# Sums of squares in one tile: DVE adds in place of products with the ones, in eight norm boundaries of a two-block transformer kernel

## Chip, cores and metric

The kernel runs on one core of one Trainium2 chip. The metric is the device time of one execution in microseconds. The kernel before has a median of 3141.66 us over three runs (3138.09 to 3142.01).

PE is the matrix engine (TensorE), DVE the vector engine, ACT the scalar engine, POOL is GpSimd; SP issues the DMAs. Each engine carries out its own instructions in the order in which the program put them, and waits where one of them needs something that another engine has not finished.

## What is computed

Two blocks of two layers each work on 512 tokens of width 1024. Each layer is a mixer and then an FFN, with a norm ahead of each and a norm behind it. The mixers (attention over chosen keys beside a chunked mLSTM in block 1; compressed, selected and windowed attention beside stick-breaking attention in block 2) play no part in the change. What matters is the frame around them:

```python
def rms_norm(x, w):
    y = x * lax.rsqrt(jnp.mean(x * x, axis=-1, keepdims=True) + EPS)
    return y * w

for l in range(DEPTH):
    h = rms_norm(x, mix_norm_pre[l]) * (1.0 + sc_m) + sh_m
    y = hybrid_mixer(h, ...)
    x = x + g_m * rms_norm(y, mix_norm_post[l])
    h = rms_norm(x, ffn_norm_pre[l]) * (1.0 + sc_f) + sh_f
    y = swiglu(h, w_gate_up[l], w_down[l])
    x = x + g_f * rms_norm(y, ffn_norm_post[l])
```

Block 2 has the same frame without scale, shift and gate (`sc`, `sh`, `g`). So between two stages there stands a boundary: the norm of y (the stage's result), the addition to x, and the norm of x for the next stage. There are eight boundaries: four after mixers and four after FFNs. The last one has no norm of x, since nothing follows it.

## The kernel before

Activations are kept with the features on the partitions: x is eight tiles of 128 features by 512 tokens in 32-bit floats, and so is y. Each weight product is done as three: the weights and the activations are split into a high part and a low part, and high by high, low by high and high by low are summed (`mm3`, which calls `self.matmul`, L303). In the views, `whi` and `wlo` are the parts of a weight: `load` fetches it by a DMA on SP, ACT copies it to `whi` (L263) and DVE subtracts to make `wlo` (L265), 128x1024 or less at a time. `hh` and `hl` are the parts of the normed x.

A mean over the features is a sum over the partitions and over eight tiles. The sum over the partitions is a product with a 128x128 tile of ones, `nrm<-...,ones` in the views, which leaves the sum on all 128 partitions. Each such product is recorded as two passes.

At a boundary the tokens are worked in two halves of 256 (`HALVES`), so that the first half can be normed while PE works on the second half of the stage's last products:

- `out_proj` (after a mixer) and `down2` (after an FFN) make y tile by tile. For each tile the square is taken on ACT (`sqy`) and added by DVE into a running tile `ssy`, except for the last of the eight tiles, whose square stays in its own tile `sql`. After a mixer ACT copies y and squares it straight from PSUM (L514, L516); after an FFN DVE first adds y to an earlier part (L1098) and ACT squares the sum (L1100).
- `post_norm` (L485) takes one half. One product with the ones over `ssy` and one over `sql` give the sum of squares of y; ACT turns it into `rstd` by Ln and Exp (L273); DVE then makes eight `yn` (L498) and adds them to x (L499).
- `squares` (L443) follows for the same half: ACT squares the eight tiles of x (L448), DVE adds them in pairs (L450), which leaves four tiles.
- `pre_norm` (L455) takes the four tiles by four products with the ones, makes `rstd` on ACT, and then `xn` on DVE (L468), `hh` on ACT (L470 or L472) and `hl` on DVE (L478 or L483).
- `norms` sets where these steps stand among the products of the stage: the first half's norm of y at the start of the second half's products, the first half's norm of x `LA` = 4 (mixer) or `LB` = 3 (FFN) weight tiles later, the second half's norm of y behind the last of them. The second half's norm of x is put off into the next stage (`self.pending`, run in `fm_split`), behind the first of its weight tiles.

The framework's scheduler gives the final order on each engine from priorities. `load` raises the priority of its DMA, its copy and its subtraction (`high_priority`), so that weights' copies come to stand between the steps of a norm. Tile names carry a number in the orders below.

Of the kernel before, what the change touches and what calls it, by code (L numbers as in the profile page):

```python
# [14 lines left out]
ALU = mybir.AluOpType  # L15
# [26 lines left out]
PH1 = 0  # L42
PH2 = 0
PXM = 0
SA = 0
LA = 4
LAG = 3
LOA = 40
# [136 lines left out]
class Net:  # L185
# [256 lines left out]

    def squares(self, hs):  # L443

        nc, x, res = self.nc, self.x, []
        for k in range(KT):
            s2 = self.half("sq")
            nc.scalar.activation(s2, x[k][:, hs], AF.Square)  # L448
            if k % 2:
                nc.vector.tensor_tensor(s2, res[-1], s2, ALU.add)  # L450
                res.pop()
            res.append(s2)
        return res

    def pre_norm(self, hs, sqs, gs, sh, hh, hl):  # L455

# [28 lines left out]
    def post_norm(self, hs, y, sqs, g, end=False):  # L485

        nc = self.nc
        ps = self.ps("nrm")
        if SA:
            nc.vector.tensor_tensor(sqs[0][:, hs], sqs[0][:, hs], sqs[1][:, hs], ALU.add)  # L490
# [1260 lines left out]
```

## Time and profile before

| | |
|---|---|
| median of 3 runs | 3141.66 us (3138.09 to 3142.01) |
| profiled execution | 3140.83 us |
| its span on the core | 3139.1 us |
| PE busy | 97%, 16196 instructions |
| DVE busy | 64%, 3692 instructions |
| ACT busy | 49%, 2758 instructions |
| mean granted clock of PE | 0.984 |

The span is what the profiler saw between the first and the last instruction. Busy time of one engine overlaps with that of the others. A timeline row gives the start in us from the span's start, the time that the instruction took (or a run of equal ones, with their count after the x), the engine, line and operation, what is written from what, and in brackets how long the engine had been idle before it and which instruction ended that. The granted clock is told as a part of full speed: 1.00 is 2.4 GHz, 0.50 is 1.2 GHz.

### The profile page before, as it was taken

How to read it: one execution, taken by the hardware profiler on the slowest of the kernel's cores; microseconds unless marked ns; L12 is line 12 of the kernel's file. 1: busy time of each engine (PE TensorE's matmuls, PEld its weight loads, DVE VectorE, ACT ScalarE, POOL GpSimd, SP SyncE). 2: the span in 40 equal slices, each digit the busy share in tenths (PEclk: the TensorE clock that was granted, in tenths of full speed). 3: DMA queues.
4: the chain of work that ended last, by engine and by line, in shares of the span. 5: the costliest groups of instructions: out<-in, count | busy, mean ns of one | idle time of the engine just before them, and what ended most of it. 6: DMA issues, size and time to landing. Idle time of an engine off the chain costs nothing.

```text
span 3139.1 us, 42582 instructions
## 1 busy us (share of the span) xinstructions
PE 3033.7 (97%) x16196; PEld 2533.5 (81%) x16196; DVE 2012.8 (64%) x3692; ACT 1545.5 (49%) x2758; POOL 66.7 (2%) x179
## 2 busy tenths in 40 slices
PE   7998999999999999999999999999999999999998
PEld 6774788889875798888988779888898877898887
DVE  6888575547787572336677677735576766775465
ACT  4445642235445652324477655534455866554343
POOL 0000000000000000000000100000000001000000
PEclk8997999999998999999999999999999999999999
DMA  7344366645322232324411124333343112342323
GB/s 236 96 137 167 101 222 196 208 141 163 112 93 69 87 125 85 110 84 158 127 61 41 61 69 151 109 97 101 97 163 107 35 48 74 114 135 83 113 82 110
DMA packets 118925, 358.40 MB, mean 114 GB/s; under 512 B 15408, under 2 KB 28464, under 8 KB 118720
## 3 DMA queue, kind: packets, MB, share of 16 engines
q1 hardware_dynamic: 118720, 355.68, 34.8%
q8 instruction: 127, 2.08, 0.3%
q14 instruction: 78, 0.64, 0.1%
HBM read 336.19 MB, written 8.42 MB: 110 GB/s over the span
## 4 chain that ended last, share of the span: by engine, by line
PE 68%; issue 17%; DVE 10%; ACT 3%; DMA 1%; POOL 1%; SPq 0%; POOLq 0%; DVEq 0%; ACTq 0%
PE ps L303 29%; PE op L303 12%; PE pj L303 9%; PE dn L303 8%; PE po L303 3%; PE tk L303 2%; DVE wlo L265 2%; PE nrm L303 1%; PE pt L306 1%; DVE yn L498 1%; DVE ss L1495 1%; DVE x L499 1%; DVE ia L846 1%; ACT whi L263 1%; DVE m L845 1%
## 5 line engine op out<-in xcount | busy, mean ns | idle before, releaser
L265 DVE TENSOR_TENSOR wlo<-raw,whi 128x1024 fp32r<-128x1024 f32 (+1 forms) x562 | 628.6, 1123 | 556.4 <-ACT whi L263 553.4
L263 ACT ACTIVATE whi<-raw 128x1024 fp32r<-128x1024 f32 (+1 forms) x562 | 549.4, 980 | 779.9 <-PE ps L303 210.7
L303 PE MATMUL ps<-hh,wlo 128*128 128x512 f32 (+1 forms) x1560 | 570.6, 366 | 0.2 <-DVE wlo L265 0.2
L303 PE MATMUL ps<-hl,whi 128*128 128x512 f32 (+1 forms) x1560 | 570.8, 367 | 0.1
L303 PE MATMUL ps<-hh,whi 128*128 128x512 f32 (+1 forms) x1560 | 570.3, 367 | 0.0
L303 PE MATMUL pj<-hh,whi 128*128 128x512 f32 (+1 forms) x944 | 352.9, 375 | 15.9 <-ACT hh L670 8.4
L303 PE MATMUL pj<-hl,whi 128*128 128x512 f32 (+1 forms) x944 | 351.4, 373 | 6.5 <-DVE hl L478 3.4
L303 PE MATMUL pj<-hh,wlo 128*128 128x512 f32 (+1 forms) x944 | 350.7, 372 | 0.0
L303 PEld LDWEIGHTS ps<-hh,wlo 128*128 128x128 f32 x1560 | 294.1, 189 | 48.7 <-DVE wlo L265 1.0
L303 PEld LDWEIGHTS ps<-hl,whi 128*128 128x128 f32 x1560 | 294.2, 189 | 48.5 <-DVE hl L478 0.4
L303 PEld LDWEIGHTS ps<-hh,whi 128*128 128x128 f32 x1560 | 293.2, 189 | 48.7 <-ACT whi L263 0.4
L303 PEld LDWEIGHTS pj<-hh,whi 128*128 128x128 f32 x944 | 179.4, 191 | 55.3 <-ACT hh L670 10.4
L303 PEld LDWEIGHTS pj<-hl,whi 128*128 128x128 f32 x944 | 180.2, 191 | 36.7 <-DVE hl L478 4.4
L303 PEld LDWEIGHTS pj<-hh,wlo 128*128 128x128 f32 x944 | 180.2, 191 | 30.1 <-issue 1.2
L649 DVE CUSTOM_DVE_ANT_0 wm<-wm,cact 128x1024 f32<-128x1024 f32 x96 | 117.0, 1222 | 107.2 <-DMA wm<-in_w_mod_dram 106.7
L303 PE MATMUL op<-hidh,wlo 128*128 128x256 f32 (+1 forms) x572 | 176.8, 309 | 1.4 <-DVE wlo L265 1.4
L303 PE MATMUL op<-hidh,whi 128*128 128x256 f32 (+1 forms) x572 | 177.1, 310 | 0.0
L303 PE MATMUL op<-hidl,whi 128*128 128x256 f32 (+1 forms) x572 | 175.8, 307 | 0.0
L303 PE MATMUL dn<-hidh,whi 128*128 128x512 f32 x352 | 136.9, 389 | 0.0
L303 PE MATMUL dn<-hidl,whi 128*128 128x512 f32 x352 | 136.9, 389 | 0.0
L303 PE MATMUL dn<-hidh,wlo 128*128 128x512 f32 x352 | 136.9, 389 | 0.0
L273 ACT ACTIVATE p<-p,st 128x128 f32<-128x128 f32 (+3 forms) x192 | 106.2, 556 | 56.0 <-DVE st L888 36.8
(350 smaller groups left out, 5782.8 us busy)
## 6 DMA issues: line engine op xcount, KB each, us to landing
raw<-in_w_in_dram SPq DMA_DIRECT2D x134, 512.0 KB, 3.4
raw<-in_w_up_dram SPq DMA_DIRECT2D x100, 512.0 KB, 3.5
wm<-in_w_mod_dram SPq DMA_DIRECT2D x96, 512.0 KB, 4.5
raw<-in_w_gu_dram SPq DMA_DIRECT2D x94, 512.0 KB, 3.5
raw<-in_w_dn_dram SPq DMA_DIRECT2D x80, 512.0 KB, 3.6
raw<-in_w_out_dram SPq DMA_DIRECT2D x52, 512.0 KB, 3.6
raw<-in_w_dn_dram SPq DMA_DIRECT2D x80, 192.0 KB, 3.2
hp<-rp SPq DMA_DIRECT2D x96, 64.0 KB, 2.0
```

What stands on the lines that cost most here:

```text
L263: nc_.scalar.activation(hi[:, :n], raw[:, :n], AF.Copy)
L265: (self.lo_eng or nc_.vector).tensor_tensor(lo[:, :n], raw[:, :n], hi[:, :n].bitcast(F32), ALU.subtract)
L273: j = self.nc.scalar.activation(out, in_, func, **kw).ins
L303: return self.paced(self.nc.tensor.matmul(*args, **kw))
L306: return self.paced(self.nc.tensor.transpose(*args))
L498: nc.vector.scalar_tensor_tensor(t, y(k, hs), g[:, k:k + 1], r, ALU.mult, ALU.mult)
L499: (nc.gpsimd if PXM >> k & 1 else nc.vector).tensor_tensor(self.x[k][:, hs], self.x[k][:, hs], t, ALU.add)
L649: self.nc.vector.tensor_tensor_reduce(raw, raw, self.cact, 1.0, 0.0, ALU.mult, ALU.add, self.mod[l][:, c:c + 1])
L845: nc.vector.max(m8, a[:, :n])
L846: nc.vector.match_replace(a[:, :n], m8, a[:, :n], GONE)
L1495: nc.vector.tensor_tensor_scan(s[:, c][:, ::-1], a[:, c][:, ::-1], a[:, c][:, ::-1], 0.0, ALU.add, ALU.bypass)
```

## The change

`SA` becomes 1, so that `post_norm` takes the branch that adds `sql` into `ssy` on DVE and makes one product. `squares` keeps one running total: the first square is written into it, and each of the other seven is added to it by DVE, so that `pre_norm` gets one tile and makes one product. Nothing else is edited.

```diff
-SA = 0
+SA = 1
...
     def squares(self, hs):
 
-        nc, x, res = self.nc, self.x, []
+        nc, x, total = self.nc, self.x, self.half("sq")
         for k in range(KT):
-            s2 = self.half("sq")
+            s2 = self.half("sq") if k else total
             nc.scalar.activation(s2, x[k][:, hs], AF.Square)
-            if k % 2:
-                nc.vector.tensor_tensor(s2, res[-1], s2, ALU.add)
-                res.pop()
-            res.append(s2)
-        return res
+            if k:
+                nc.vector.tensor_tensor(total, total, s2, ALU.add)
+        return [total]
```

The lines behind `squares` move up by two: L498 becomes L496, L499 becomes L497, L516 and L518 become L514 and L516.

PE has 15608 rows in its order before and 15550 after; DVE has 3576 and 3634. The orders of SP and POOL are the same. Three places show how it moves.

The first is PE's order at the first half of the norm of y, at the boundary after the mixer of block 1, layer 0. `op` is a tile of the mixer's last product, `ch` and `cl` are the parts of what goes into it. Before:

```order
L303 MATMUL op_3414<-ch_3094,wlo_3410 128x256
L303 MATMUL nrm_3441<-ssy_3131,ones 128x256
L303 MATMUL op_3491<-ch_3095,whi_3409 128x256
L303 MATMUL op_3491<-cl_3103,whi_3409 128x256
L303 MATMUL op_3491<-ch_3095,wlo_3410 128x256
L303 MATMUL nrm_3441<-sql_3132,ones 128x256
L303 MATMUL op_3491<-ch_3096,whi_3409 128x256
```

After:

```order
L303 MATMUL op_3414<-ch_3094,wlo_3410 128x256
L303 MATMUL nrm_3441<-ssy_3131,ones 128x256
L303 MATMUL op_3494<-ch_3095,whi_3409 128x256
L303 MATMUL op_3494<-cl_3103,whi_3409 128x256
L303 MATMUL op_3494<-ch_3095,wlo_3410 128x256
L303 MATMUL op_3494<-ch_3096,whi_3409 128x256
```

The one product stands where the product over `ssy` stood; three products of weights that stood ahead of the product over `sql` now stand behind it.

The second is DVE's order at the first half of the norm of x, at the boundary after the mixer of block 2, layer 0, from the last addition to x on. Before:

```order
L499 TENSOR_TENSOR x_18084<-x_18084,yn_18379 128x256
L265 TENSOR_TENSOR wlo_18572<-raw_18570,whi_18571 128x1024
L450 TENSOR_TENSOR sq_18384<-sq_18382,sq_18384 128x256
L450 TENSOR_TENSOR sq_18389<-sq_18387,sq_18389 128x256
L450 TENSOR_TENSOR sq_18394<-sq_18392,sq_18394 128x256
L265 TENSOR_TENSOR wlo_18607<-raw_18605,whi_18606 128x1024
L450 TENSOR_TENSOR sq_18399<-sq_18397,sq_18399 128x256
L518 TENSOR_TENSOR ssy_18042<-ssy_18042,sqy_18428 128x256
```

After:

```order
L450 TENSOR_TENSOR sq_18382<-sq_18382,sq_18384 128x256
L265 TENSOR_TENSOR wlo_18572<-raw_18570,whi_18571 128x1024
L450 TENSOR_TENSOR sq_18382<-sq_18382,sq_18387 128x256
L516 TENSOR_TENSOR ssy_18042<-ssy_18042,sqy_18431 128x256
L450 TENSOR_TENSOR sq_18382<-sq_18382,sq_18390 128x256
L516 TENSOR_TENSOR ssy_18042<-ssy_18042,sqy_18460 128x256
L450 TENSOR_TENSOR sq_18382<-sq_18382,sq_18393 128x256
L450 TENSOR_TENSOR sq_18382<-sq_18382,sq_18396 128x256
L265 TENSOR_TENSOR wlo_18607<-raw_18605,whi_18606 128x1024
L450 TENSOR_TENSOR sq_18382<-sq_18382,sq_18399 128x256
L516 TENSOR_TENSOR ssy_18042<-ssy_18042,sqy_18495 128x256
L450 TENSOR_TENSOR sq_18382<-sq_18382,sq_18402 128x256
```

Four adds of pairs have become seven adds into the total `sq_18382`, with two low parts and three `ssy` adds of the second half among them. PE has 96 other products between the first half's product of y and its product of x at the mixers' boundaries, 100 at the FFNs'.

The third is DVE's order at the second half of the norm of x, at the same boundary, from the last addition to x on. Before:

```order
L499 TENSOR_TENSOR x_18084<-x_18084,yn_18700 128x256
L450 TENSOR_TENSOR sq_18705<-sq_18703,sq_18705 128x256
L450 TENSOR_TENSOR sq_18710<-sq_18708,sq_18710 128x256
L265 TENSOR_TENSOR wlo_18930<-raw_18928,whi_18929 128x1024
L450 TENSOR_TENSOR sq_18715<-sq_18713,sq_18715 128x256
L450 TENSOR_TENSOR sq_18720<-sq_18718,sq_18720 128x256
L265 TENSOR_TENSOR wlo_19032<-raw_19030,whi_19031 128x1024
```

After:

```order
L497 TENSOR_TENSOR x_18084<-x_18084,yn_18700 128x256
L450 TENSOR_TENSOR sq_18703<-sq_18703,sq_18705 128x256
L265 TENSOR_TENSOR wlo_19032<-raw_19030,whi_19031 128x1024
L450 TENSOR_TENSOR sq_18703<-sq_18703,sq_18708 128x256
L450 TENSOR_TENSOR sq_18703<-sq_18703,sq_18711 128x256
L450 TENSOR_TENSOR sq_18703<-sq_18703,sq_18714 128x256
L450 TENSOR_TENSOR sq_18703<-sq_18703,sq_18717 128x256
L450 TENSOR_TENSOR sq_18703<-sq_18703,sq_18720 128x256
L450 TENSOR_TENSOR sq_18703<-sq_18703,sq_18723 128x256
```

Six of the seven adds stand in a row, each on the total that the one before it wrote. The low part of the weight `18930` has moved ahead of the first `yn`, and its copy on ACT between Ln and Exp, as at the other three mixers' boundaries. Between the second half's product of y and its product of x, PE now has 74 other products at the mixers' boundaries and 53 at the FFNs'.

## Rows read from the trace of the kernel before

**Rows 1.** The profile page: engines' busy time, the chain by engine, one group (mean ns).

```profile
PE 3033.7 (97%) x16196; PEld 2533.5 (81%) x16196; DVE 2012.8 (64%) x3692; ACT 1545.5 (49%) x2758; POOL 66.7 (2%) x179
...
PE 68%; issue 17%; DVE 10%; ACT 3%; DMA 1%; POOL 1%; SPq 0%; POOLq 0%; DVEq 0%; ACTq 0%
...
L649 DVE CUSTOM_DVE_ANT_0 wm<-wm,cact 128x1024 f32<-128x1024 f32 x96 | 117.0, 1222 | 107.2 <-DMA wm<-in_w_mod_dram 106.7
```

**Rows 2.** PE's timeline at a second half's norm of x, mixer of block 2.

```profile
1948.06 1.89 PE L303 MATMUL nrm<-sq,ones 128*128 128x256 f32 x8
...
1949.90 0.28 PE L303 MATMUL ps<-hl,whi 128*128 128x256 f32 x1
1950.02 0.28 PE L303 MATMUL ps<-hh,wlo 128*128 128x256 f32 x1
```

**Rows 3.** Timeline of all engines at a first half's norm of y, after a mixer.

```profile
368.71 0.59 PE L303 MATMUL nrm<-ssy,ones 128*128 128x256 f32 x2
...
369.19 0.38 ACT L516 ACTIVATE sql<-op 128x256 f32<-128x256 f32 x1
...
369.62 0.30 PEld L303 LDWEIGHTS nrm<-sql,ones 128*128 128x128 f32 x2 [0.17 <-ACT sql L516]
```

**Rows 4.** The same view at a first half's norm of y, after an FFN.

```profile
738.36 0.59 PE L303 MATMUL nrm<-ssy,ones 128*128 128x256 f32 x2
...
739.02 0.42 ACT L1100 ACTIVATE sql<-y 128x256 f32<-128x256 f32 x1 [2.46 <-DVE y L1098]
```

**Rows 5.** DVE's timeline, and a row of PE's, up to the first half's norm of x.

```profile
377.17 1.22 DVE L265 TENSOR_TENSOR wlo<-raw,whi 128x1024 fp32r<-128x1024 f32 x1
378.31 1.09 DVE L450 TENSOR_TENSOR sq<-sq,sq 128x256 f32<-128x256 f32 x3
379.31 1.22 DVE L265 TENSOR_TENSOR wlo<-raw,whi 128x1024 fp32r<-128x1024 f32 x1
...
380.79 1.48 DVE L518 TENSOR_TENSOR ssy<-ssy,sqy 128x256 f32<-128x256 f32 x3
...
381.30 1.89 PE L303 MATMUL nrm<-sq,ones 128*128 128x256 f32 x8
```

**Rows 6.** PE's timeline ahead of a second half's norm of y, FFN of block 2.

```profile
2306.46 0.39 PE L303 MATMUL pj<-hl,whi 128*128 128x256 f32 x1 [0.89 <-DVE hl L478]
```

**Rows 7.** Timeline of all engines, second half, after a mixer of block 2.

```profile
1937.56 0.59 PE L303 MATMUL nrm<-sql,ones 128*128 128x256 f32 x2
...
1938.19 0.47 ACT L273 ACTIVATE rstd<-nrm,eps 128x256 f32<-128x256 f32 x1 [1.36 <-PE nrm L303]
...
1939.15 0.88 DVE L498 SCALAR_TENSOR_TENSOR yn<-y,par,rstd 128x256 f32<-128x256 f32 x2 [1.06 <-ACT rstd L273]
...
1939.50 1.06 ACT L263 ACTIVATE whi<-raw 128x1024 fp32r<-128x1024 f32 x1 [0.38 <-PE pj L303]
...
1945.02 0.75 DVE L450 TENSOR_TENSOR sq<-sq,sq 128x256 f32<-128x256 f32 x2
```

**Rows 8.** Timelines of PE and DVE, second half, after an FFN of block 2.

```profile
2309.16 0.59 PE L303 MATMUL nrm<-sql,ones 128*128 128x256 f32 x2
...
2310.97 0.87 DVE L498 SCALAR_TENSOR_TENSOR yn<-y,par,rstd 128x256 f32<-128x256 f32 x2
...
2316.82 0.75 DVE L450 TENSOR_TENSOR sq<-sq,sq 128x256 f32<-128x256 f32 x2
...
2317.29 1.13 PE L303 MATMUL nrm<-sq,ones 128*128 128x256 f32 x4 [0.60 <-DVE sq L450]
```

**Rows 9.** PE's timeline after two waits; then stretches: length, engines' busy time, PE clock.

```profile
91.08 0.79 PE L303 MATMUL ua<-cqh,whi 128*128 128x512 f32 x1 [3.75 <-ACT cqh L252]
...
2566.49 0.77 PE L306 MATMUL pt<-ident,ss 128*128 128x128 f32 x3 [2.53 <-ACT ss L273]
...
91.20:94.60 3.40, 3.40 (x8) 2.38 (x9) 3.40 (x6) 1.69 (x3) 0.00 (x0) 0.50 0.10 39
2566.67:2570.09 3.42, 3.42 (x13) 2.68 (x13) 2.92 (x5) 2.52 (x5) 1.25 (x3) 0.50 0.01 2
```

## Prediction

> **What bounds the kernel now.** I read the profile page first, for the busy shares and the chain that ended last [rows 1]. PE is busy 97% of the span and holds 68% of the chain, with 17% of issue time beside it; DVE is busy 64% but has only 10% of the chain. So a product taken off PE is worth its whole slot, and work given to DVE costs nothing as long as PE has other products in hand until DVE is done. Which of the two holds has to be read at the 29 places where a changed product stands. I therefore read PE's, ACT's and DVE's timelines around a norm after a mixer and around one after an FFN, for both halves of the tokens, and set the two orders of instructions beside them. PE issues in order: a product that waits for a sum holds up everything behind it, however much other work is ready.
>
> **What is removed.** The norm of y is taken in 8 places with two halves each, and loses one product in each: 16. The norm of x is taken in 14 halves (the last boundary has none) and loses three in each: 42. The order has 58 rows fewer on PE and 58 more on DVE. A product with the ones costs more than one of the weights' products. Eight recorded passes, four products, take from 1948.06 to 1949.90; less one ordinary step of 0.12 that is 1.72, so 0.43 us each [rows 2]. Removed: 58 x 0.43 = **-24.9 us**, all on PE.
>
> **First half of the norm of y.** Before, the product over ssy runs at 368.71, three products of the last tile cover ACT's square of sql, and the second product follows it at 369.62 with a wait of 0.17 [rows 3]. The one product now stands where the first stood, but needs ACT's square (done at 369.57) and a DVE add after it. An add costs 0.42: three that don't depend on each other take 1.09 us and the next instruction starts 1.00 after them, 0.33 for each step, so 1.09 - 2 x 0.33 = 0.42 [rows 5]. From a square to its reader 0.05 pass [rows 3]. So PE waits until 369.57 + 0.05 + 0.42 + 0.05 = 370.09, or 1.38; 0.17 of it was paid before: 1.2. After an FFN y is added by DVE and squared after that: 739.44 + 0.52 = 739.96 against 738.36, or 1.6 [rows 4]. Four of each: 4.8 + 6.4 = **+11.2 us**. Below this lies 0.5 for each place, if only the add were new; above it 2, if a weight's low part stands before the add.
>
> **First half of the norm of x.** DVE is free of the x adds at 377.17, which becomes 377.64 with the later product of y [rows 5]. From there the new order has seven adds, two low parts of weights (1.14 each, 377.17 to 378.31) and three ssy adds before the product can start. With 0.36 for an add, between the 0.33 of free ones and the 0.53 of chained ones (three of ssy take 1.48 = 0.42 + 2 x 0.53), that is 3.6 + 2.3 = 5.9, so the sum is there at 383.6. PE reached its four products at 381.30 [rows 5]; it now comes at about 370.09 + 0.43 + 96 x 0.12 = 382.0. It waits 1.5, four times. After an FFN 100 other products stand between and y adds fill the gaps of the chain; I take 0.4 three times, between 0 and the mixer's 1.5. Together **+7.2 us** (6 to 11).
>
> **What DVE's longer queue delays.** Behind the adds stand the next xn and hl, the other weights' low parts and the second half of y. After an FFN PE already waits 0.89 for hl [rows 6], so nothing covers a further delay there: I take 1.0 three times, the three chained adds of 0.33 each that are new. After a mixer PE has more in hand: 0.5 four times. The last norm of all waits for sql already and gets one add in its path: 0.5. Together **+5.5 us** (0 to 12).
>
> **Second half of the norm of x: the main term.** After a mixer the path before is: last product of y at 1937.56, Ln at 1938.19 (0.63 later), yn at 1939.15, adds of squares from 1945.02, so 5.87 for yn and x [rows 7]. In the new order a weight's copy on ACT (1.06) stands between Ln and Exp, and its low part on DVE (1.14) before yn: 0.63 + 0.47 + 1.06 + 1.14 = 3.3 from product to yn. Then 5.87. Then the adds: one (0.34), a low part (1.14), and six that each need the one before: 5 x 0.53 + 0.42 + 0.05 = 3.1, together 4.6. Sum 13.8 us. PE meanwhile has the one product and, by the new order, 74 others: 0.43 + 74 x 0.12 = 9.3. It waits 4.5, four times, and 1.2 more at the first boundary, where one of the modulation's products on DVE stands among the adds [rows 1]: 19.2. After an FFN PE waits already, 0.60 for the first pair sums [rows 8]. There yn comes 1.81 after the last y product, the adds 5.85 after that, and 4.6 follow: 12.3 against 0.43 + 53 x 0.12 = 6.8. The wait is 5.5, and 6.6 at the two boundaries where one more low part stands among the adds: 18.7, less 3 x 0.6 paid before, 16.9. Together **+36 us**. If the six chained adds cost 0.34 each it is 7 x 1.0 less, 29; if more weight copies stand in the path, some 1.1 each, 44.
>
> **The clock.** After PE had waited 3.75 us, the next 3.40 us ran at a granted clock of 0.50, which is the 1.2 GHz level, and so did 3.42 us after a wait of 2.53 [rows 9]. Waits of 4.5 to 6.6 us in seven places are longer than both, and are followed by dense products. 3.4 us at half speed loses 1.7; seven times is 12, of which I take **+11 us**, as a slower PE also shortens the next wait for hl. Bounds: 0, and 22 if each lasts twice as long. The Trainium skill, page "TensorE: Matmul & The Clock Gate", section "HAM oscillation — how this bites in real kernels", says that a wait between groups of products makes the next group start cold, which speaks against this change. Trace and rule agree; with it the sum is the forecast, without it 11 us lower.
>
> **Sum.** -24.9 + 11.2 + 7.2 + 5.5 + 36 + 11 = +46 us on the profiled execution of 3140.83, whose span is 3139.1. That execution stands 0.8 below the median of 3141.66: about **3187 us**. SP's and POOL's orders are unchanged, and ACT has the same number of instructions, so no term stands for them. What these measurements can tell from no change is about 0.2%, 6.3 us.
>
> **Rivals.**
> Clock stays full: the seven waits come, but PE goes on at 2.4 GHz: 3187 - 11 = 3176. For it: PE had been dense before each wait. Against it: [rows 9]. 28%.
> Clock falls for twice as long: 3187 + 11 = 3198. For it: after a long wait products meet more waits, for xn and hl. 12%.
> Adds are covered, so faster: DVE idles 36% of the span; if it takes each square as ACT delivers it, in the second half of the norm of x, the sums are done when PE comes. Only the first-half wait for y is left: -24.9 + 11.2 = -13.7, 3128 us. It decides where a wait is under 13.7/14 = 1 us in each of the 14 halves. Against it: before, the adds begin only when DVE has done all its x adds [rows 7], and the order after keeps that. 4%.
> Nearly no change: the main term is cut to 1 us, if PE's cover in the second half were 14 us in place of 7 to 9; then -24.9 + 11.2 + 7.2 + 5.5 + 1 = 0, 3142. Nothing in the order gives such cover. 4%.
> That the change does nothing is excluded: the 58 rows are gone from PE's order and the product reads the one running total.
>
> **How the numbers follow.** The forecast has 52%. The range holds it with the clock's rivals: down to 3164, where the clock stays full (11 less), the main term is 29 (7 less) and DVE's longer queue delays nothing (5 less); up to 3207, where the clock falls for twice as long (11 more) and the main term is 44 (8 more). Faster than 3135 has 4%, within 0.2% 4%, slower 92%.
>
> **What would show it.** In the changed kernel's trace: 116 fewer passes on the ones; the product over ssy waiting 1.3 to 1.6 for a DVE add in eight first halves; the product over sq waiting 4 to 7 us for DVE's add in seven second halves and 1 to 2 us in four first halves; chained adds 0.53 apart; a clock of 0.50 behind the long waits. I am wrong if PE's idle time in front of the ones' products grows by less than 25 us, or if DVE's adds end before PE comes.

## The result and the profile after

The changed kernel takes 3197.0 us (median of five runs, 3191.6 to 3198.7), against 3140.2 before (now five runs, where three had given 3141.66): a ratio of 1.0177, 95% interval 1.0166 to 1.0188. By the medians that is 57 us slower, by the ratio 56. The forecast was 3187, and the range of 3164 to 3207 holds the result. The profiled execution has a span of 3189.8 us, 50.7 longer than the one before. It lies at the fast end of the runs, so a ledger made from it falls some 6 us short of the medians.

First the page of the changed kernel, to be set beside [rows 1]: busy time and the chain by engine.

```profile
PE 3023.5 (95%) x16080; PEld 2526.8 (79%) x16080; DVE 2036.4 (64%) x3750; ACT 1547.4 (49%) x2758; POOL 66.0 (2%) x179
...
PE 64%; issue 16%; DVE 12%; DMA 5%; ACT 3%; POOL 1%; SPq 0%; DVEq 0%; POOLq 0%; ACTq 0%
```

The 116 passes are gone from PE, and 58 instructions have come to DVE. PE is busy for 10 us less in a span that is 51 longer, though products worth 25 us were taken off it by the estimate of 0.43 each. DVE's share of the chain rose by two points only; that of DMA rose from 1% to 5%, which no term of the prediction had.

The view of PE's waits says where the time went. Its rows give PE's line, the engine and line waited for, the total in us, how often, and the longest. Of the changed kernel:

```profile
PE nrm L303 <- DVE sq L450: 40.3, 11, 6.1
...
PE nrm L303 <- DVE ssy L488: 11.9, 9, 1.4
```

Before, the same products waited 1.9 us for the squares of x and 0.5 for those of y. The two new waits together are 52 us, twice what the removed products were worth.

These are the waits themselves, on PE's timeline: at the boundary after the mixer of block 2, layer 0 (first half of y, first half of x, second half of x), and then for an FFN (first half of y, second half of x).

```profile
1941.61 0.70 PE L303 MATMUL nrm<-ssy,ones 128*128 128x256 f32 x2 [1.21 <-DVE ssy L488]
...
1955.15 0.67 PE L303 MATMUL nrm<-sq,ones 128*128 128x256 f32 x2 [1.33 <-DVE sq L450]
...
1983.90 0.79 PE L303 MATMUL nrm<-sq,ones 128*128 128x256 f32 x1 [4.10 <-DVE sq L450]
...
2317.33 0.70 PE L303 MATMUL nrm<-ssy,ones 128*128 128x256 f32 x2 [1.42 <-DVE ssy L488]
...
2361.42 1.22 PE L303 MATMUL nrm<-sq,ones 128*128 128x256 f32 x2 [6.08 <-DVE sq L450]
```

Where a row has x1 the two passes stand in two rows. Before, the third of these places had no wait at all, and the fifth had 0.60 [rows 2, 8]. PE's, ACT's and DVE's timelines at the third place show why it takes so long.

```profile
1970.16 0.66 PE L303 MATMUL nrm<-ssy,ones 128*128 128x256 f32 x2
...
1970.86 0.47 ACT L273 ACTIVATE rstd<-nrm,eps 128x256 f32<-128x256 f32 x1 [0.52 <-PE nrm L303]
1971.23 1.05 ACT L263 ACTIVATE whi<-raw 128x1024 fp32r<-128x1024 f32 x1
1972.18 0.41 ACT L273 ACTIVATE rstd<-rstd 128x256 f32<-128x256 f32 x1
...
1973.46 0.87 DVE L496 SCALAR_TENSOR_TENSOR yn<-y,par,rstd 128x256 f32<-128x256 f32 x2
...
1979.31 0.42 DVE L450 TENSOR_TENSOR sq<-sq,sq 128x256 f32<-128x256 f32 x1
1979.65 1.22 DVE L265 TENSOR_TENSOR wlo<-raw,whi 128x1024 fp32r<-128x1024 f32 x1
1980.78 3.06 DVE L450 TENSOR_TENSOR sq<-sq,sq 128x256 f32<-128x256 f32 x6
```

Between Ln and Exp stands the weight's copy of 1.05 us. From the product at 1970.16 to the first yn are 3.3 us, to the first add 5.85 more, and the six chained adds take 3.06, which is 0.42 + 5 x 0.53. Each of these three is within 0.1 of its term in the prediction.

Last, the stretches with a lower granted clock at the seven second-half waits: length in us; busy time of PE, PEld, DVE, ACT and POOL, with the number of instructions; PE's granted clock; DMA share and GB/s. Behind their sum stand the first parts of two of them, and one more stretch, at another place.

```profile
412.30:419.00 6.70, 5.88 (x25) 5.70 (x26) 6.33 (x15) 4.34 (x9) 0.00 (x0) 0.50 0.69 223
794.60:797.90 3.30, 3.08 (x12) 2.91 (x13) 1.03 (x4) 1.24 (x3) 0.41 (x2) 0.50 0.02 6
1139.40:1146.10 6.70, 5.33 (x23) 5.15 (x24) 4.22 (x11) 4.01 (x8) 0.00 (x0) 0.50 0.14 55
1514.80:1524.90 10.10, 6.05 (x26) 5.87 (x27) 7.41 (x19) 3.33 (x8) 1.04 (x2) 0.50 0.45 144
1982.40:1989.10 6.70, 5.20 (x22) 5.02 (x23) 4.22 (x11) 3.82 (x8) 0.00 (x0) 0.50 0.17 67
2357.90:2364.60 6.70, 3.18 (x13) 3.01 (x14) 4.01 (x9) 1.34 (x4) 0.42 (x1) 0.50 0.74 247
2825.50:2828.80 3.30, 3.30 (x18) 3.30 (x17) 2.46 (x7) 3.24 (x7) 0.00 (x0) 0.50 0.00 0
...
sum 43.50, PE 32.03 PEld 30.96 DVE 29.70 ACT 21.31 POOL 1.88; mean PE 4.58 PEld 4.42 DVE 4.24 ACT 3.04 POOL 0.27
...
1514.80:1518.80 4.00, 0.00 (x0) 0.00 (x0) 3.58 (x8) 0.00 (x0) 0.00 (x0) 0.50 0.86 259
2357.90:2361.30 3.40, 0.00 (x0) 0.00 (x0) 2.98 (x6) 0.00 (x0) 0.00 (x0) 0.50 1.02 314
...
1501.10:1504.40 3.30, 3.30 (x18) 3.30 (x17) 2.83 (x8) 1.14 (x3) 0.00 (x0) 0.50 0.72 222
```

All seven stand at 0.50, the 1.2 GHz level, for 43.5 us in all. Six of them begin before the wait is over, by 0.2 to 4 us, and PE's idle 11.5 us in them are the ends of these same waits; no further wait stands in them. PE did 32 us of work in them, 3.1 to 6.1 behind each wait, which at 2.4 GHz would have taken 16. The last row stands behind two waits for hl, of 1.23 and 0.89 us, that ended at 1498.88 and 1500.75; the kernel before has no such stretch at that boundary.

### The profile page after: what moved, and what is told of

Same layout as the page of the kernel before. It is cut to its first block, busy times and chain, and to the rows that moved or that the text cites. A ratio compares the mean times of both kernels' runs of the same rounds, so it can differ in the third digit from the quotient of the medians.

```text
span 3189.8 us, 42475 instructions
## 1 busy us (share of the span) xinstructions
PE 3023.5 (95%) x16080; PEld 2526.8 (79%) x16080; DVE 2036.4 (64%) x3750; ACT 1547.4 (49%) x2758; POOL 66.0 (2%) x179
## 4 chain that ended last, share of the span: by engine, by line
PE 64%; issue 16%; DVE 12%; DMA 5%; ACT 3%; POOL 1%; SPq 0%; DVEq 0%; POOLq 0%; ACTq 0%
PE ps L303 26%; PE pj L303 11%; PE op L303 10%; PE dn L303 6%; DMA wm<-in_w_mod_dram 3%; PE tk L303 3%; PE po L303 2%; DVE wlo L265 2%; DVE yn L496 1%; PE pt L306 1%; PE nrm L303 1%; DVE x L497 1%; DVE wm L647 1%; DVE sq L450 1%; ACT whi L263 1%
## 5 line engine op out<-in xcount | busy, mean ns | idle before, releaser
L303 PE MATMUL pj<-hh,whi 128*128 128x512 f32 (+1 forms) x944 | 353.0, 376 | 15.3 <-ACT hh L668 8.4
L303 PEld LDWEIGHTS pj<-hh,whi 128*128 128x128 f32 x944 | 179.8, 191 | 54.8 <-ACT hh L668 10.5
```

The costliest lines, as they stand in the source:

```text
L303: return self.paced(self.nc.tensor.matmul(*args, **kw))
```

## The experiments

Each is the kernel before or the changed kernel with the edit shown (`...` marks lines left out). Times are medians beside runs of the kernel before on the same chip; the difference is taken from the ratio.

### The three parts of the change, each alone

The norm of y alone:

```diff
-SA = 0
+SA = 1
```

> The norm of y alone is changed (one product in place of two, 16 adds); the norm of x keeps its four pair sums. Theory (a saved product is worth 0.43 us, a wait of PE costs what it lasts): 16 products give back 6.9 us, eight first-half waits of 1.21 to 1.42 us cost 10.5, the last norm of all about 1: 5 us slower than before, 3145 us. Rival (each of the 58 new adds costs the same, since DVE is what is late): 16 of 58 parts of 57 us, 16 us slower, 3156 us.

Measured: 3150.7 us, ratio 1.0032 (1.0021 to 1.0044), 10 us slower. The row of PE's waits for the sums of y is the changed kernel's, 11.9 us in 9 waits. The other 5 us of loss, which the theory lacked, are in the FFN of block 1, layer 0: PE's view of waits for that stretch, empty before, has this one row, and around its end 6.6 us stand at a granted clock of 0.50.

```profile
PE dn L303 <- ACT hidh L252: 3.5, 1, 3.5
```

The running total in one half only (first `HALVES[1]`, then `HALVES[0]`), the pair sums in the other:

```diff
+        one = hs is HALVES[1]
         for k in range(KT):
...
+            if one and k:
+                nc.vector.tensor_tensor(res[0], res[0], s2, ALU.add)
+                continue
```

> The running total is used in the seven second halves of the norm of x alone, all else as before. Theory: 21 products give back 9 us, the seven waits in front of the product cost 34, the clock behind them some 20: 45 us slower than before, 3185 us. Rival (equal cost for each add): 21 of 58 parts of 57 us, 21 us slower, 3161 us.

Measured: 3168.5 us, ratio 1.0084 (1.0071 to 1.0096), 26 us slower. The theory missed by 19, the rival by 5, but neither's reason holds: the loss is not spread over the adds, since PE's waits for the sums of x are 25.7 us, and FFN boundaries have 4.8 to 5.7 of it each. What the theory had wrong is the mixers, with 2.3 to 2.4 in place of 4.1 to 5.2. ACT's timeline, at the place shown above for the changed kernel:

```profile
1955.32 0.48 ACT L273 ACTIVATE rstd<-nrm,eps 128x256 f32<-128x256 f32 x1 [1.36 <-PE nrm L303]
1955.83 0.42 ACT L273 ACTIVATE rstd<-rstd 128x256 f32<-128x256 f32 x1
1956.63 1.06 ACT L263 ACTIVATE whi<-raw 128x1024 fp32r<-128x1024 f32 x1 [0.38 <-PE pj L303]
```

Here no weight's copy stands between Ln and Exp. Nor does one in the runs with the norm of y alone or with the total in the first halves alone, at the same place; it comes there where the parts are made together. So the parts are not independent: with the others the second half's wait is longer by 1.8 us at three of the four mixers, and by 2.7 at the first. Which of them brings the copy in stays open, since no run has two of the three.

> The running total is used in the seven first halves of the norm of x alone, all else as before. Theory: 21 products give back 9 us, four waits of 1.33 after the mixers cost 5.3, DVE's longer queue about 3: no change within 4 us, 3140 us. Rival (equal cost for each add): 21 us slower, 3161 us.

Measured: 3160.4 us, ratio 1.0061 (1.0048 to 1.0073), 19 us slower. My theory fell here. The wait after a mixer is 2.94 us and not 1.33:

```profile
1935.32 1.22 PE L303 MATMUL nrm<-sq,ones 128*128 128x256 f32 x2 [2.94 <-DVE sq L451]
```

In the changed kernel PE is held up by 1.21 at the norm of y ahead of this place, and so arrives later at the sum of x: part of the longer wait is the same loss in another place, but how much was not timed. Another part is behind the adds: at the FFN boundaries PE now waits for a weight's low part in the stage's last products, where it waited 0.34 in the kernel before.

```profile
1468.90 0.39 PE L303 MATMUL op<-hidh,wlo 128*128 128x256 f32 x1 [0.91 <-DVE wlo L265]
```

The three ratios together (0.32 + 0.84 + 0.61) make 1.77%, the whole loss. That they agree so well is luck, since the parts are not independent: with the whole change the second-half waits are 35.0 us in place of 25.7, and the four first-half waits 5.3 in place of 11.7.

### Is it the wait, or the clock behind it?

In the changed kernel, products whose result is overwritten, in front of the second half's product over the total:

```diff
+        if hs is HALVES[1]:
+            self.second = getattr(self, "second", 0) + 1
+            for j in range(32 if self.second & 1 else 42):
+                self.matmul(ps[:, :256], self.ones_r, hh[j & 7][:, HALVES[0]], start=True, stop=True)
```

> The changed kernel with 32 (after a mixer) or 42 (after an FFN) products of ready tiles put in front of the second-half product over the total; their result is overwritten. They take 3.8 and 5.0 us, which is less than PE waits there, so the sum comes no earlier and no later, but PE isn't idle. Theory (the part of the loss that the waits don't explain, some 24 us, is mostly a clock that falls behind them): the stretches at 0.50 behind these seven places go, and the kernel is some 20 us faster than the changed one, 3177 us. Rival (that part is work that DVE's longer queue delays, the clock is paid anyway): the same time as the changed kernel, 3197 us within 4.

Measured: 3174.5 us, ratio 1.0107 (1.0092 to 1.0122): 22 us faster than the changed kernel by the ratios (12 between the two profiled executions), with 254 more products on PE. The stretch behind the wait after the mixer of block 2, layer 0, at 0.50 above, reads:

```profile
1974.70:1981.50 6.80, 6.80 (x53) 6.49 (x54) 5.22 (x15) 5.08 (x11) 0.00 (x0) 1.00 0.01 2
```

The 4 to 5 us behind the other six waits stand at 1.00 too. So idleness costs twice here: what PE waits, and then the slow stretch. For the latter the changed kernel's rows give 16 us and this run 22, with some us of doubt.

### The chain of adds, and their number

The seven adds as a tree:

```diff
...
+            n = 1
+            while stack and stack[-1][1] == n:
+                nc.vector.tensor_tensor(s2, stack.pop()[0], s2, ALU.add)
+                n *= 2
+            stack.append((s2, n))
+        return [stack[0][0]]
```

> The changed kernel with the seven adds of a norm of x as a tree (pairs, pairs of pairs, one sum) in place of a running total: as many adds on DVE and as many products, but two adds at the end wait for the one before in place of five in a row. Theory (the number of adds behind the last addition to x, with the copies among them, makes the sum late; that each needs the one before adds 0.2 us a step): some 0.6 us less at each of seven waits, about 4 us faster than the changed kernel, 3193 us. Rival (the dependence from add to add is what costs): the waits fall to the half and the clock with them, 20 us or more faster, 3177 us.

Measured: 3188.4 us, ratio 1.0154 (1.0136 to 1.0172), some 7 us faster than the changed kernel; the two intervals overlap, so the size is uncertain, but not that most of the loss stays. The second-half waits are 0.6 to 0.7 shorter at all seven places (3.38 in place of 4.10, 5.44 in place of 6.08), as expected; the four waits in first halves after mixers are gone, and PE's waits for the sums of x fall from 40.3 us to this:

```profile
PE nrm L303 <- DVE sq L451: 30.2, 7, 5.4
```

The dependence from add to add is the smaller part. The rest is, by the rows above, where the adds stand: behind all additions to x, with a low part among them. That is read from the timeline; no run has moved them on DVE.

### More cover for the first half

> As the run with the total in the first halves alone, but after a mixer the first half's norm of x stands one weight tile later among PE's products (LA 5 in place of 4), so that PE has 24 more products in hand, 2.9 us. Theory (the wait is the sum's time less PE's cover): the four waits of 2.94 us after mixers go, and the clock that fell behind two of them; 14 us faster than that run, 3146 us, still no faster than the kernel before because of what DVE's longer queue delays after the FFNs. Rival (DVE's load itself costs, wherever the product stands): no faster than 3158 us.

The edit is that of the total in the first halves, and `LA` = 5. Measured: 3152.9 us, ratio 1.0041 (1.0027 to 1.0055), 13 us slower than before and about 6 better than with `LA` = 4. PE's waits for the four sums are gone, but of the 14 us expected only 6 came back. PE now stands a little later, at the hl of the next stage, where it did not wait before, at all four mixers:

```profile
1940.95 0.39 PE L303 MATMUL pj<-hl,whi 128*128 128x256 f32 x1 [1.51 <-DVE hl L482]
```

Both expectations fall between: the wait is the sum's time less PE's cover, as the theory says, but cover taken ahead of the product is missing behind it.

### The adds on another engine

```diff
-SA = 1
+SA = 0
...
-                nc.vector.tensor_tensor(total, total, s2, ALU.add)
+                nc.gpsimd.tensor_tensor(total, total, s2, ALU.add)
```

> The running total of the norm of x is added on GpSimd in place of DVE, in all halves; the norm of y is as before the change. DVE loses even the 56 pair adds. GpSimd is busy 2% of the span; a one-input operation of 128x256 takes it 0.41 to 0.51 us, the time of an add is not known. Theory (the sum is late because the adds stand behind all additions to x in DVE's queue; squares come from ACT at about 0.73 us a tile): with an add below 0.73 us the sum is there about 1 us after the last square, the waits after mixers go, and the 42 products saved are worth 18 us: 3125 us. Rival (an add on GpSimd takes 1 us or more, or slows DVE's own): seven adds in a row end later than DVE's did, 3150 us or more.

Measured: 3219.2 us, ratio 1.0249 (1.0232 to 1.0267), the slowest of all. The rival is right, by its second arm: an add on GpSimd takes 0.80 us (median), but seven of them in a row 7.67 here, and they slow DVE down. DVE's and POOL's timelines at a second half after a mixer:

```profile
1988.49 0.88 DVE L496 SCALAR_TENSOR_TENSOR yn<-y,par,rstd 128x256 f32<-128x256 f32 x2
1989.28 0.76 DVE L497 TENSOR_TENSOR x<-x,yn 128x256 f32<-128x256 f32 x2
1989.95 1.85 DVE L496 SCALAR_TENSOR_TENSOR yn<-y,par,rstd 128x256 f32<-128x256 f32 x2
1991.72 1.84 DVE L497 TENSOR_TENSOR x<-x,yn 128x256 f32<-128x256 f32 x2
...
1989.81 7.67 POOL L450 TENSOR_TENSOR sq<-sq,sq 128x256 f32<-128x256 f32 x7 [22.51 <-ACT sq L448]
```

From the moment at which POOL begins, two yn take 1.85 us in place of 0.88, and two additions to x 1.84 in place of 0.76.

### Why the loss grows within an FFN

Within the FFN of block 1, layer 0, the changed kernel's instructions fall 5.4 us further behind those of before, though no norm stands there: its first product into `pj` starts at 430.69, 7.0 us later than before, and its first into `op` at 708.55, 12.4 later. (The expectations below put this at 6.7.) Of the chain of waits between 395 and 735 us, transfers of the modulation's weights (`wm`) have 27% in the changed kernel and 1% in the one before. DVE multiplies these in its own order, among the weights' low parts, and waits 106 us for them between 420 and 735 us, 98 before. The test leaves 48 of the modulation's 96 products out of both kernels; the scale, shift and gate of layer 1 in block 1 are zero there.

```diff
+        if l == 1:
+            self.nc.vector.memset(self.mod[l][:, c:c + 1], 0.0)
+            return
```

> The kernel before, with the 48 products of layer 1's modulation in block 1 left out (a small write of zeros in their place), so that DVE has no transfer of 512 KB to wait for in the FFN of block 1, layer 0. Base for the next run. No theory depends on its time alone; DVE waits there 107 us for such transfers before, PE hardly at all, so it should be within 10 us of the kernel before, rather faster.

> The changed kernel with the same 48 products left out. Theory (6 to 7 us of the loss come in the FFN of block 1, layer 0, where DVE works at the pace of those transfers and can't make up a late start): the difference to the run before it is 50 us in place of 57, and between 430 and 733 us PE loses less than 1.5 us more than there, in place of 6.7. Rival (that loss comes from something else, such as ACT's order or the place of the weights' copies): the difference stays at 57 us, and PE loses over 5 us in that stretch.

Measured: 3139.9 us for the kernel before without them (ratio 0.9999, 0.9990 to 1.0008), 3189.8 for the changed one (1.0153, 1.0136 to 1.0170). The difference is 48 us by the ratios and 50 by the medians, in place of 56 and 57, which is a drop with some us of doubt; and between the same two products the changed kernel loses nothing against its base (6.8 us behind at both), in place of 5.4. PE's waits there, of the changed kernel with the modulation:

```profile
PE ps L303 <- DVE wlo L265: 3.0, 4, 1.5
PE dn L303 <- ACT hidh L252: 0.5, 1, 0.5
PE dn L303 <- DVE hidl L253: 0.2, 1, 0.2
```

Without it this view is empty for both kernels. The theory holds so far: the loss in this stage hangs on the modulation's products on DVE, and a DVE that comes late to it does not make it up. The run takes out 48 products of 1.22 us together with their transfers, so it does not show that the pace of the transfers, and not DVE's work on them, is the cause. The 106 us that DVE waits speak for the transfers.

### The opposite of the change

No adds and eight products, in the first halves and then in the second:

```diff
-            if k % 2:
+            if k % 2 and not (hs is HALVES[0]):
```

> The change's opposite in the first halves of the norm of x: no adds, eight products with the ones; all else as before. 28 products more cost 12 us. Theory (each add on DVE in a first half costs PE some 0.8 us by what stands behind it in DVE's queue, as three more cost 2.3 a boundary in the run with the product one tile later): 28 adds less give back up to 21 us, 3141 + 12 - 21 = 3132 us at best, and 3141 if only the half of it comes back. Rival (DVE has room, only PE's products count): 3153 us.

> The change's opposite in the second halves of the norm of x: no adds, eight products with the ones; all else as before. 28 products more cost 12 us; the waits of 0.6 to 0.7 us at two FFN boundaries go, and xn and hl come up to 1.3 us sooner at seven places. Theory (PE is short of work there, so that DVE's chain sets the time): 3141 + 12 - 1 - 9 = 3143 us. Rival (only PE's products count): 3153 us.

Measured: 3147.6 us (1.0026, 1.0017 to 1.0035) and 3146.9 us (1.0021, 1.0011 to 1.0030). Of the 12 us that the 28 products cost by the estimate of 0.43 each, 4 to 5 come back in either case, as DVE has less in its queue. The second run is within 4 us of its theory; the first gave back less than the half that the theory asked for at least. So both directions lose, and of the splits tried the four pair sums are the best. None of the runs that do all the work was faster than the kernel before.

## Why the prediction was right, and where its terms were off

**Removed products, -24.9 us.** Right in number, 58. A slot of 0.43 each was not timed by itself; the runs with 28 products more, 6.6 and 8.2 us slower though DVE had less to do, don't contradict it.

**First half of the norm of y, +11.2.** Four waits of 1.21 and four of 1.42: 10.5.

**First half of the norm of x, +7.2.** Four waits of 1.33 after mixers, where 1.5 was forecast, and none at the product after FFNs, where 0.4 was forecast: 5.3.

**Second half of the norm of x, +36.** After mixers 5.2, 4.2, 4.1 and 4.1, where 5.7 and three times 4.5 were forecast; after FFNs 5.3, 6.1 and 6.1 for 5.5, 6.6 and 6.6. That is 35.0, less the 1.9 paid before: 33.1. The main term was right to 3 us, and for its reason: both the copy between Ln and Exp and the six chained adds stand in the trace as forecast.

**The clock, +11.** Mis-sized; with the FFN below, this is the step that put the forecast low. The sum took 3.4 us of work at 0.50 for each of seven waits. In the trace PE did 3.1 to 6.1 us of work at 0.50 behind each, 4.6 on average; the loss is 16 us by the rows and 22 by the run with products in the wait. The 3.4 was read from too short a window: the first stretch of [rows 9] ends at 94.60, but the clock stood at 0.50 from before the end of that wait, at 91.08, to 95.3. (Its second stretch, of 3.42, is whole.)

```profile
88.70:91.00 2.30, 0.00 (x0) 0.00 (x0) 1.56 (x3) 2.27 (x4) 0.00 (x0) 0.50 0.48 142
91.10:95.30 4.20, 4.20 (x9) 3.08 (x10) 4.20 (x7) 1.79 (x3) 0.00 (x0) 0.50 0.10 40
```

The rival in which the clock falls for twice as long came nearest to the median, at 3198 us, and I gave it 12% against 52% for the forecast. That is luck in part. What spoke for it, that PE meets further waits right behind a long one, is not what the rows show: no further wait stands in these stretches. And some 5 us of what the forecast missed are the FFN's below, which that rival did not have either. The rival in which the clock stays full is refuted. The rule of the Trainium skill (page "TensorE: Matmul & The Clock Gate", section "HAM oscillation — how this bites in real kernels"), that a wait makes the next group start cold, held at all seven places.

**What DVE's longer queue delays, +5.5.** Too small, and with a place missing. The waits for hl behind the boundaries grew by 3.6 us in all (5.1 to 8.7) and the last norm by 0.9, about as forecast. Not forecast were the 5.4 us in the FFN of block 1, layer 0: the prediction used the row of `wm` for its duration only and passed over the 107 us that DVE waits for these transfers [rows 1]. Before, PE had no recorded wait in that stage at all, but by a small margin: the run with the norm of y alone already brought one of 3.5 us.

**The sum.** With the measured sizes it is -24.9 + 10.5 + 5.3 + 33.1, then 16 to 22 for the clock, 3.6 + 0.9 for hl and the last norm, and 5.4 for that FFN: 50 to 56 us, against 51 in the profiled execution and 57 by the medians, where +46 was forecast. The clock and the FFN are what was too small, by 5 to 11 and by 5 us; the three terms of waits were taken 5 us too large, and that these partly cancel is luck. Nor is the ledger as exact as it looks: in the mixer of block 1, layer 1, PE's instructions of the changed kernel come 3.4 us nearer to those of before (18.8 behind at 955 us, 15.3 at 1045), which no term has.

**Faster, with the adds covered:** refuted at 11 places.

## What to carry to other kernels

Work moved from the busiest engine to an idle one is free only where the busy engine has other work in hand until the result is there; count that work from the order of instructions, place by place, against the whole path of the result, and not against the other engine's share of busy time. A wait of 4 to 6 us on TensorE here cost another 2 to 3 in the slow stretch behind it, so filling it with products of no use won back 22 us. Before an engine that is off the critical path gets more work, look for a stage in which it already waits for transfers between its own instructions: a late start was not made up in such a stage here.

## What was not expected of the hardware

**GpSimd and DVE slow each other.** Beside GpSimd's adds, DVE's two-input operations on 128x256 took about twice as long (a pair of yn 1.85 us in place of 0.88), and GpSimd's own adds 1.10 on average (7.67 for seven) in place of the median of 0.80. The Trainium skill has a rule for this, page "SBUF — State Buffer", section "SBUF: two separate sides": DVE operations with two inputs in SBUF and GpSimd operations that read SBUF share a pair of ports, and one waits while the other holds it. These rows agree with it; my expectation for that run had it only as a rival, without a price.

**The clock can fall before a wait is over, and not at the same point of it.** The same kind of wait, 4.1 us after a mixer of block 2, was followed by 5.2 us of work at 0.50 in layer 0, where the clock had fallen 1.5 us before the wait ended, and by 3.3 us in layer 1, where it was still at 1.00 when the product began. Shorter waits had it too, but not each time: with the total in the second halves alone, the product behind waits of 2.3 to 2.4 us after mixers was followed by work at 0.50 in three of four places. What decides it, these runs do not show.
